# SwiGLU and output products of a decoder layer: 512 weight columns moved past stationary activations, inner rows transposed on TensorE, residual stream and norms token-major

## The chip, the cores and the metric

One core of a Trainium2 chip runs the kernel. The metric is the time of one execution on the device in microseconds (us), the median of three runs. The names used below: TensorE (PE in the profile) multiplies matrices, with PEld for its loads of the stationary operand; VectorE (DVE), ScalarE (ACT) and GpSimd (POOL) work element by element; SyncE (SP) issues the DMA transfers, in order, from one queue.

## What is computed

One decoder layer on 256 tokens of width 2048, conditioned on a vector c, everything in f32:

```
cond = silu(c);  mod = cond @ ada_w + ada_b          # nine vectors of 2048: shift, scale, gate, three times
h = rmsnorm(x)*g*(1+sc1) + sh1
x = x + 0.5*gt1 * swiglu(h, gate, up, down)          # inner width 5632
h = rmsnorm(x)*g*(1+sc2) + sh2
x = x + gt2 * (mixer(h) @ w_out)                     # 8 attention heads, 8 gated delta rule heads
h = rmsnorm(x)*g*(1+sc3) + sh3
x = x + 0.5*gt3 * swiglu(h, gate, up, down)
out = rmsnorm(x)*final_norm
swiglu(h, wg, wu, wd) = (silu(h @ wg) * (h @ wu)) @ wd
```

## The kernel before

**Weights.** All weight matrices are cut into 5392 tiles of 128x128 and packed on the host in the order in which the kernel uses them. The class `Stream` brings eight tiles at a time: a block of 512 KB by DMA (L91), ScalarE's cast to a rounded part `whi` (L93), and VectorE's difference `wlo` (L105). Three blocks of each kind are in memory, and in the SwiGLUs every fourth block lies in a buffer of its own. A product of weights and activations is three products of such parts: hi with hi, hi with lo, lo with hi.

**Feature-major layout.** The residual stream `x` lies with features on partitions: 16 slices of 128 features, 256 tokens each. `hs` holds the modulated input in the same layout, hi and lo beside each other. A weight tile is the stationary operand, and the tokens move past it: `mm` (L380 to 382) moves 512 columns (hi and lo of 256 tokens) past `whi`, then 256 past `wlo`; the output bank holds hi in its first half and the lo product in its second, and `merge` (L384) adds the halves with a ScalarE copy and a VectorE addition. The first part of the first SwiGLU (`gate_up_first`, L449 to 451) and the mixer's `project` (L623 to 625) move 256 columns three times for each tile and need no merge. Only `project_rows` in the mixer (L636 to 638, tile `pv`) has the other form: 128 tokens of `hs` stationary, 512 weight columns moving.

**Stages.** The first SwiGLU runs in two parts of 28 and 16 slices of the inner width (`PARTS`), each with gate and up (`pgu`, then `pg` and `pu`) and down (`pd`); the mixer with its projections (`pp`, `pv`) and small products; the output projection (`po`); the second SwiGLU in two parts of 22 and 22. The inner rows `hid` come out of gate and up feature-major, as down needs them.

**Conditioning.** The nine vectors `mod` are made column by column (128 features, 1 MB of weights, called an ada column here) by one VectorE product and sum (L233). `Stream.next` calls for such a column at a pace that the table `RATE` gives for each block number.

**Residual and norms.** `residual` (L405, L406) adds a 128-feature slice, scaled with its gate column. `sumsq_add` squares it on ScalarE and sums on GpSimd; `norm_rstd` (L282 to 309) sums over partitions with TensorE (`nsum`), takes a root and one refining step, and spreads the result over a row with TensorE (`nrow`). `modulate_one` (L313) then makes `hs`, slice by slice, `AHEAD` of the products. `final` scales 16 slices and stores them.

The framework's scheduler sets each engine's order from the program's order and its own estimates; transfers are tied to the last weight block by `issue_after(W.last)`.

Of the kernel before, what the change touches and what calls it, by code (L numbers as in the profile page):

```python
# [22 lines left out]
PARTS = ((0, 28, NF), (0, NF // 2, NF))  # L23
CHUNKS = (0, 2, 8, 16)
LEAD = (2, 5, 5)
NH = 8
# [7 lines left out]
RATE = ((0, 0.5), (24, 0.34), (56, 0.45), (68, 0.06), (112, 0.5), (168, 0.38), (264, 0.1), (280, 0.25), (408, 0.125))  # L34
# [6 lines left out]
HIDX = 3  # L41
# [4 lines left out]
MAGIC = 0x5F3759DF  # L46

# [3 lines left out]
for _k, _w in (  # L51
    ("foxm", 384), ("mL", 128), ("mU", 128), ("zm", 2 * 64), ("blk", 4), ("id16", 16),
    ("tri", 128), ("tri64", 128), ("tru64", 128), ("sgn", GR),
):
    CST[_k] = (_n, _w)
    _n += _w
# [12 lines left out]
class Stream:  # L69


    def __init__(self, nc, w, raw, hi, lo):
# [6 lines left out]
        self.at, self.first = {}, []  # L79

# [14 lines left out]

    def next(self, mat, k, n, width=1):
        i = len(self.order)
        if i % WB == 0:
# [7 lines left out]
            if b in self.at:  # L106
                self.at.pop(b)()
# [11 lines left out]
def layer_kernel(ctx: ExitStack, tc: tile.TileContext, xt, xrow, c, adaw, cols, cst, w, out, order, dbg=None):  # L119
# [67 lines left out]
    for b, sl in X_LATE.items():  # L187
        W.at[b] = lambda sl=sl: x_late(*sl)
# [16 lines left out]
    mod = keep.tile([P, 9 * KD], F32, name="mod")  # L205
# [6 lines left out]
    def ada_col():  # L212
# [56 lines left out]
    def sumsq_add(j):  # L269

        if j == 0:
            sqa["acc"] = tmp.tile([P, T], F32, name="sqacc", bufs=1)
            A.activation(sqa["acc"], x[:, j], AF.Square)
            return
        s = tmp.tile([P, T], F32, name="sq")
        A.activation(s, x[:, j], AF.Square)
        if j == KD - 1:
            sqa["src"] = [sqa["acc"], s]
        else:
            G.tensor_tensor(sqa["acc"], sqa["acc"], s, ALU.add)  # L280

    def norm_rstd(keep_row=False):  # L282

        ps = psf("nsum")
        src = sqa["src"]
        for i, s in enumerate(src):
            for t in range(2):
                PE.matmul(ps[:, t * 2 : t * 2 + 2], s[:, t * P : (t + 1) * P], L("ones", 0, 2),
                          start=(i == 0 and t == 0), stop=(i == len(src) - 1), skip_group_check=True)
        y = tiny.tile([P, 2], F32, name="nstd")  # L290
        hv = tiny.tile([P, 2], F32, name="nhv")
        ya = tiny.tile([P, 2], F32, name="nya")
        A.activation(y, ps[:, 0:4:2], AF.Sqrt, bias=L("eps"), scale=1.0 / D)
        V.tensor_scalar(hv, ps[:, 0:4:2], -0.5 / D, -0.5 * EPS, ALU.mult, ALU.add)
        V.reciprocal(y, y)
        V.tensor_tensor(ya, y, y, ALU.mult)
        V.tensor_tensor(ya, ya, hv, ALU.mult)
        V.scalar_tensor_tensor(y, ya, 1.5, y, ALU.add, ALU.mult)
        rb = tmp.tile([P, 2, P], F32, name="rb", bufs=1)
        pr = psf("nrow")  # L300
        for t in range(2):
            last = V.tensor_scalar(rb[:, t], L("ones"), y[:, t : t + 1], None, ALU.mult)
            PE.matmul(pr[:, t * P : (t + 1) * P], rb[:, t], ident, start=True, stop=True)
        W.held = ([None, sqa["hold"]] if sqa["hold"] is not None else []) + [last.ins]
        if not keep_row:
            return pr[:, :T]
        row = tmp.tile([P, T], F32, name="nrow", bufs=1)
        V.tensor_copy(row, pr[:, :T])
        return row

    hs = keep.tile([P, KD, 2, T], F32R, name="hs")

    def modulate_one(j, g1, sh, r):  # L313

        t = pt("ht")
# [17 lines left out]
    def modulate(which, m_sh, m_sc):  # L333
        ada_need(max(m_sh, m_sc), KD - 1)
        g1 = gains(which, m_sc, 0, KD)
        r = norm_rstd()
        hq["next"], hq["one"] = 0, lambda j: modulate_one(
            j, g1[:, j : j + 1], mod[:, m_sh * KD + j : m_sh * KD + j + 1], r)
# [872 lines left out]
```

## Time and profile before

| what | us |
|---|---|
| median of the runs | 2098.63 (2095.85 to 2101.67) |
| profiled execution, span | 2101.9 |
| first SwiGLU, up to the gap ahead of the mixer | 0 to 789.1 |
| mixer projections | 795.4 to 1223.2 |
| output projection | 1223.2 to 1331.6 |
| second SwiGLU | 1338.6 to 2085.7 |
| end | 2085.7 to 2101.9 |

The profile of one execution gives the span from the first to the last instruction; the execution's own time outside it isn't given apart, and the span stands 3.3 us above the median. The page shows busy time for each engine, the chain that ended last, and groups of instructions by line and tile; the trace can be asked for stretches and for single instructions with their starts. Starts of neighbouring matmuls say more than their durations, since matmuls overlap.

### The profile page before, as it was taken

Reading aid. Unit: us, or ns where it says so; the run is one execution under the profiler, and the core shown is the slowest. Engines: PE = TensorE matmul, PEld = TensorE weight load, DVE = VectorE, ACT = ScalarE, POOL = GpSimd, SP = SyncE. Lnnn points to the kernel's source line nnn. Section 1 sums busy time; section 2 is a strip of 40 time slices with the busy share of each in tenths; the row PEclk is TensorE's granted clock in tenths of the full one; section 3 lists DMA queues with packets and bytes.
Section 4 is the critical chain, followed back from the end, with each engine's and each line's share of the span. In section 5 each row is a group of like instructions: output and inputs, shape, how many; then the busy total and the mean of one; then the engine's idle time right before and its main releaser. Section 6 shows DMA issues by size and latency. Waiting matters only on the chain.

```text
span 2101.9 us, 33335 instructions
## 1 busy us (share of the span) xinstructions
PE 2037.6 (97%) x12935; PEld 1825.4 (87%) x12935; DVE 1564.1 (74%) x2393; ACT 1014.9 (48%) x1583; POOL 65.0 (3%) x58
## 2 busy tenths in 40 slices
PE   7999999999999999889999999999999999999997
PEld 5999999888888888779989978788888888888886
DVE  6898977888888988877878878866666555555554
ACT  5534544333444446646656654554444334444442
POOL 0000000000000120000000002000000000000011
PEclk9999999999999999999999999999999999999998
DMA  9988767999888875776666567666676555555553
GB/s 385 330 306 317 284 209 258 362 341 362 333 328 335 324 290 175 209 253 212 223 226 231 200 217 279 207 237 232 235 238 219 186 185 191 184 187 191 185 186 111
DMA packets 130064, 523.36 MB, mean 249 GB/s; under 512 B 16489, under 2 KB 21609, under 8 KB 111729
## 3 DMA queue, kind: packets, MB, share of 16 engines
q1 hardware_dynamic: 129906, 521.23, 69.7%
q8 instruction: 102, 1.67, 0.3%
q14 instruction: 56, 0.46, 0.1%
HBM read 516.83 MB, written 4.34 MB: 248 GB/s over the span
## 4 chain that ended last, share of the span: by engine, by line
PE 89%; DVE 5%; DMA 3%; issue 1%; ACT 1%; SPq 0%; DVEq 0%; POOL 0%; ACTq 0%; POOLq 0%
PE pd L381 15%; PE pu L381 11%; PE pg L381 11%; PE pd L382 8%; PE pg L382 5%; PE pu L382 5%; PE pgu L451 5%; PE pgu L449 5%; PE pgu L450 4%; PE pp L623 3%; PE pp L625 3%; PE pp L624 3%; PE po L381 2%; DVE wlo L105 2%; DMA adat<-in_ada_dram 1%
## 5 line engine op out<-in xcount | busy, mean ns | idle before, releaser
L105 DVE TENSOR_TENSOR wlo<-wraw,whi 128x1024 fp32r<-128x1024 f32 x674 | 823.7, 1228 | 344.0 <-ACT whi L93 341.4
L93 ACT CAST whi<-wraw 128x1024 fp32r<-128x1024 f32 x674 | 701.7, 1047 | 682.2 <-issue 173.7
L381 PE MATMUL pd<-hid,whi 128*128 128x512 f32 x1408 | 497.0, 397 | 0.0
L382 PE MATMUL pd<-hid,wlo 128*128 128x256 f32 x1408 | 396.0, 281 | 0.8 <-DVE wlo L105 0.7
L233 DVE CUSTOM_DVE_ANT_0 adat<-adat,cs,colt 128x2048 f32<-128x2048 f32 x140 | 329.7, 2355 | 29.3 <-DMA adat<-in_ada_dram 29.1
L381 PE MATMUL pg<-hs,whi 128*128 128x512 f32 x960 | 342.5, 397 | 2.3 <-DVE hs L324 1.8
L381 PE MATMUL pu<-hs,whi 128*128 128x512 f32 x960 | 343.2, 398 | 0.0
L381 PEld LDWEIGHTS pd<-hid,whi 128*128 128x128 f32 x1408 | 264.2, 188 | 64.7
L382 PE MATMUL pg<-hs,wlo 128*128 128x256 f32 x960 | 270.6, 282 | 0.0
L382 PE MATMUL pu<-hs,wlo 128*128 128x256 f32 x960 | 270.2, 281 | 0.0
L382 PEld LDWEIGHTS pd<-hid,wlo 128*128 128x128 f32 x1408 | 265.4, 189 | 2.5 <-DVE wlo L105 2.1
L449 PE MATMUL pgu<-hs,whi 128*128 128x256 f32 x896 | 252.6, 285 | 9.1 <-ACT hs L319 4.6
L451 PE MATMUL pgu<-hs,wlo 128*128 128x256 f32 x896 | 250.7, 285 | 3.9 <-DVE wlo L105 3.9
L450 PE MATMUL pgu<-hs,whi 128*128 128x256 f32 x896 | 253.1, 284 | 0.0
L381 PEld LDWEIGHTS pg<-hs,whi 128*128 128x128 f32 x960 | 181.0, 188 | 45.8 <-issue 2.1
L381 PEld LDWEIGHTS pu<-hs,whi 128*128 128x128 f32 x960 | 180.9, 188 | 43.8
L623 PE MATMUL pp<-hs,whi 128*128 128x256 f32 x656 | 193.0, 295 | 6.9 <-ACT whi L93 5.8
L625 PE MATMUL pp<-hs,wlo 128*128 128x256 f32 x656 | 188.9, 288 | 1.7 <-DVE wlo L105 1.7
L624 PE MATMUL pp<-hs,whi 128*128 128x256 f32 x656 | 189.1, 288 | 0.0
L382 PEld LDWEIGHTS pg<-hs,wlo 128*128 128x128 f32 x960 | 181.9, 190 | 0.0
L382 PEld LDWEIGHTS pu<-hs,wlo 128*128 128x128 f32 x960 | 181.9, 189 | 0.0
L449 PEld LDWEIGHTS pgu<-hs,whi 128*128 128x128 f32 x896 | 172.0, 193 | 10.8 <-ACT hs L319 5.0
(304 smaller groups left out, 2422.3 us busy)
## 6 DMA issues: line engine op xcount, KB each, us to landing
wraw<-in_w_dram SPq DMA_DIRECT2D x674, 512.0 KB, 4.3
adat<-in_ada_dram SPq DMA_DIRECT2D x140, 1024.0 KB, 6.6
rw<-rowd SPq DMA_DIRECT2D x24, 128.0 KB, 6.7
xr<-in_xr_dram SPq DMA_DIRECT2D x4, 512.0 KB, 5.2
adaf<-in_ada_dram SPq DMA_DIRECT2D x4, 512.0 KB, 9.3
adaf<-in_ada_dram SPq DMA_DIRECT2D x2, 1024.0 KB, 12.9
xd<-x SPq DMA_DIRECT2D x4, 512.0 KB, 6.7
x<-ld SPq DMA_DIRECT2D x16, 128.0 KB, 6.1
```

The costliest lines, as they stand in the source:

```text
L93: self.cast = self.nc.scalar.copy(self.h, r).ins
L105: nc.vector.tensor_tensor(self.l, r, self.h.bitcast(F32), ALU.subtract)
L233: V.tensor_tensor_reduce(t, t, cs, 1.0, L("adab", q, 1), ALU.mult, ALU.add, mod[:, q : q + 1])
L381: PE.matmul(ps, wt[0], act.rearrange("p a t -> p (a t)"), start=first, stop=False)
L382: PE.matmul(ps[:, :T], wt[1], act[:, 0], start=False, stop=last)
L449: PE.matmul(o, wh, hs[:, k, 0], start=first and s == 0, stop=False, skip_group_check=skip)
L450: PE.matmul(o, wh, hs[:, k, 1], start=False, stop=False, skip_group_check=skip)
L451: PE.matmul(o, wl, hs[:, k, 0], start=False, stop=last, skip_group_check=skip)
L623: PE.matmul(pp[i][:, :T], wh, hs[:, k, 0], start=(k == 0), stop=False)
L624: PE.matmul(pp[i][:, :T], wh, hs[:, k, 1], start=False, stop=False)
L625: PE.matmul(pp[i][:, :T], wl, hs[:, k, 0], start=False, stop=(k == KD - 1))
```

## The change

The residual stream `x` becomes token-major: 128 tokens on partitions, twice 2048 features. In the SwiGLUs and the output projection, 128 tokens of activations are now stationary and 512 weight columns (four tiles) move; `products` issues six matmuls for it, three for each half t of the tokens. Gate and up give token-major inner rows, so `turned` transposes them with TensorE, eight 128x128 transposes for four slices, `STEPS_BEHIND` products later, and splits them into hi and lo. `down` puts the first half of the tokens `SKEW` slices ahead in the last pass before a norm. The residual works on 512 features of one token half with a gate row `gtr`, which goes from the columns `mod` through DRAM (`row_send`, `row_load`). Sums of squares come from ScalarE's accumulator, token by token, and `modulate` scales, transposes (`pxt`) and modulates. The mixer's `project` takes `mm` and `merge`. The gates' rates and parts change (`RATE` from block 68 on, second SwiGLU in 24 and 20 slices), `x` is loaded again token-major (`x_rows`), and tables are padded so that tiles start at other addresses (`pad`, `SHIFT`). `final` scales four 512-wide pieces for each half.

```diff
-PARTS = ((0, 28, NF), (0, NF // 2, NF))
+PARTS = ((0, 28, NF), (0, 24, NF))
+LATER_LEAD = 4
+STEPS_BEHIND = 4
+SKEW = 2
+SHIFT = 8
-RATE = (..., (68, 0.06), ...)
+RATE = (..., (68, 0.15), ...)
...
+    hbuf = keep.tile([P, KD * 2 * T + 32], F32R, name="hs")
+    hview = [hbuf[:, o : o + KD * 2 * T].rearrange("p (k a t) -> p k a t", k=KD, a=2) for o in (0, SHIFT)]
...
+    def row_send(m, b):
+        g, f = ROW[m]
+        gs = tiny.tile([P, 4], F32, name="gs")
+        V.tensor_scalar(gs, mod[:, m * KD + 4 * b : m * KD + 4 * b + 4], f, None, ALU.mult)
+        with tc.issue_after(W.last):
+            nc.sync.dma_start(gdram[g, 4 * b : 4 * b + 4].rearrange("j p -> p j"), gs)
+    def row_load(m, b):
+        src = gdram[ROW[m][0], 4 * b : 4 * b + 4].rearrange("j p -> (j p)").unsqueeze(0).to_broadcast([P, 512])
+        with tc.issue_after(W.last):
+            nc.sync.dma_start(gtr[:, 512 * b : 512 * b + 512], src)
...
+    def norm_rstd(t):
+        A.activation(y, col(3), AF.Sqrt, bias=col(6), scale=1.0 / D)
+        V.scalar_tensor_tensor(hv, col(3), -0.5 / D, col(5), ALU.mult, ALU.add)
         V.reciprocal(y, y)
+        V.scalar_tensor_tensor(ya, y, hv, y, ALU.mult, ALU.mult)
         V.scalar_tensor_tensor(y, ya, 1.5, y, ALU.add, ALU.mult)
...
+        def one(j):
+            if j % 2 == 0:
+                st["ps"] = psf("pxt")
+                for t in range(2):
+                    xn = tmp.tile([P, T], F32, name="xn", bufs=4)
+                    if t:
+                        last = V.tensor_scalar(xn, X(t, j * P, T), y[t], None, ALU.mult)
+                    else:
+                        A.activation(xn, X(t, j * P, T), AF.Copy, scale=y[t])
+                    for q in range(2):
+                        o = q * T + t * P
+                        PE.transpose(st["ps"][:, o : o + P], xn[:, q * P : (q + 1) * P], ident)
...
+    def residual(ps, t, b, m_gt, squares):
+        row_need(m_gt, b)
+        sl = slice(512 * b, 512 * b + 512)
+        d = tmp.tile([P, 512], F32, name="rs")
+        V.tensor_tensor(d, ps, gtr[:, sl], ALU.mult)
+        sqa["hold"] = V.tensor_tensor(X(t, 512 * b, 512), X(t, 512 * b, 512), d, ALU.add).ins
+        if squares:
+            square(t, b)
...
+    def products(ps, hi_, lo_, wt, first, last, both=(0, 1)):
+        wh, wl = wt
+        for t in both:
+            PE.matmul(ps[t], hi_(t), wh, start=first, stop=False)
+            PE.matmul(ps[t], lo_(t), wh, start=False, stop=False)
+        for t in both:
+            PE.matmul(ps[t], hi_(t), wl, start=False, stop=last)
+        step()
...
+        def turned(c, src):
+            pz = [bank("pz") for _ in range(2)]
+            for t in range(2):
+                for q in range(4):
+                    PE.transpose(pz[t][:, q * P : (q + 1) * P], src[:, t, q * P : (q + 1) * P], ident)
+            h4 = hid[c] = hp.tile([P, 4, 2, T], F32R, name="hid", tag="hid")
+            for t in range(2):
+                A.copy(h4[:, :, 0, sl], pv)
+                V.tensor_tensor(h4[:, :, 1, sl], pv, h4[:, :, 0, sl].bitcast(F32), ALU.subtract)
...
-                wh, wl = W.next(m, k, n)
-                PE.matmul(pp[i][:, :T], wh, hs[:, k, 0], start=(k == 0), stop=False)
-                PE.matmul(pp[i][:, :T], wh, hs[:, k, 1], start=False, stop=False)
-                PE.matmul(pp[i][:, :T], wl, hs[:, k, 0], start=False, stop=(k == KD - 1))
+                mm(pp[i], W.next(m, k, n), hs[:, k], k == 0, k == KD - 1)
...
+        for t in range(2):
+            y = norm_rstd(t)
+            V.scalar_tensor_tensor(X(t, 1536, 512), X(t, 1536, 512), y, cs[:, 1536:], ALU.mult, ALU.mult)
+            A.activation(X(t, 0, 512), X(t, 0, 512), AF.Copy, scale=y)
+            V.tensor_scalar(X(t, 512, 512), X(t, 512, 512), y, None, ALU.mult)
+            A.activation(X(t, 1024, 512), X(t, 1024, 512), AF.Copy, scale=y)
+            for b in (0, 3, 1, 2):
+                nc.sync.dma_start(out[:, t, 512 * b : 512 * b + 512], X(t, 512 * b, 512))
```

How it stands on the engines, first on TensorE in the gate products of the second SwiGLU, before. The row gives line, operation, output, then the moving and the stationary operand, and the moving size (numbers tell buffers apart):

```order
L382 MATMUL pg_19850<-hs_128,wlo_19856 128x256
L381 MATMUL pg_19850<-hs_128,whi_19854 128x512
L382 MATMUL pg_19850<-hs_128,wlo_19856 128x256
L381 MATMUL pg_19850<-hs_128,whi_19854 128x512
L382 MATMUL pg_19850<-hs_128,wlo_19856 128x256
```

The same place in the changed kernel, where a group's inner rows `sg` are transposed into `pz` between two products; two `pgu` banks hold the token halves:

```order
L511 MATMUL pgu_12761<-whi_12783,hs_88 128x512
L512 MATMUL pgu_12761<-whi_12783,hs_88 128x512
L511 MATMUL pgu_12762<-whi_12783,hs_88 128x512
L512 MATMUL pgu_12762<-whi_12783,hs_88 128x512
L514 MATMUL pgu_12761<-wlo_12785,hs_88 128x512
L514 MATMUL pgu_12762<-wlo_12785,hs_88 128x512
L533 MATMUL pz_12799<-colt_93,sg_12607 128x128 x4
L533 MATMUL pz_12800<-colt_93,sg_12607 128x128 x4
L511 MATMUL pgu_12761<-whi_12816,hs_88 128x512
```

Two rows for each tile became six for four tiles, weights and activations changed places, and a batch of eight transposes stands between two products. Now VectorE between the first SwiGLU and the mixer, before (`nsum` and `rb` belong to the norm, `ht` and `hs` to the modulation):

```order
L405 SCALAR_TENSOR_TENSOR x<-pd,gh,x 128x256
L406 SCALAR_TENSOR_TENSOR x<-pd,gh,x 128x256
L105 TENSOR_TENSOR wlo<-wraw,whi 128x1024
L294 TENSOR_SCALAR nhv<-nsum 128x2
L295 RECIPROCAL nstd<-nstd 128x2
L296 TENSOR_TENSOR nya<-nstd 128x2
L297 TENSOR_TENSOR nya<-nya,nhv 128x2
L298 SCALAR_TENSOR_TENSOR nstd<-nya,nstd 128x2
L302 TENSOR_SCALAR rb<-colt,nstd 128x128 x2
L105 TENSOR_TENSOR wlo<-wraw,whi 128x1024
L316 SCALAR_TENSOR_TENSOR ht<-x,g_8163,nrow 128x256 x3
```

And in the changed kernel, from the last addition of the first token half on (`xn` is what TensorE transposes):

```order
L483 TENSOR_TENSOR x<-x,rs 128x512
L482 TENSOR_TENSOR rs<-pd,gtr 128x512
L358 SCALAR_TENSOR_TENSOR nhv<-ss 128x1
L359 RECIPROCAL nstd<-nstd 128x1
L483 TENSOR_TENSOR x<-x,rs 128x512
L360 SCALAR_TENSOR_TENSOR nya<-nstd,nhv 128x1
L113 TENSOR_TENSOR wlo<-wraw,whi 128x1024
L361 SCALAR_TENSOR_TENSOR nstd<-nya,nstd 128x1
L358 SCALAR_TENSOR_TENSOR nhv<-ss 128x1
L359 RECIPROCAL nstd<-nstd 128x1
L360 SCALAR_TENSOR_TENSOR nya<-nstd,nhv 128x1
L361 SCALAR_TENSOR_TENSOR nstd<-nya,nstd 128x1
```

The second half's addition to `x` moved behind the first half's reciprocal, a weight block's split stands inside the chain of small steps, and another follows after the first scalings.

More of the change, by code (lines that the diff above doesn't have):

```diff
@@ L40 @@
 TILE_US = 0.35
-HIDX = 3
 MORE = True
@@ L267, in sqrt_table, with square @@
         return A.activation(d, after, AF.Sqrt, scale=0.0)
[L269 to L294, printed above, removed]
+    def square(t, b):
+        j1 = tmp.tile([P, 512], BF16, name="jq")
+        A.activation(j1, X(t, 512 * b, 512), AF.Square, accum_out=ss[:, t, b : b + 1])
+        if b == 2:
+            V.tensor_reduce(ss[:, t, 4:5], ss[:, t, 0:3], mybir.AxisListType.X, ALU.add)
+            V.tensor_scalar(ss[:, t, 5:6], ss[:, t, 4:5], -0.5 / D, -0.5 * EPS, ALU.mult, ALU.add)
+            V.tensor_scalar(ss[:, t, 6:7], ss[:, t, 4:5], 1.0 / D, EPS, ALU.mult, ALU.add)
@@ L298, in norm_rstd @@
         V.scalar_tensor_tensor(y, ya, 1.5, y, ALU.add, ALU.mult)
[L299 to L311, printed above, removed]
+        return y
     def modulate_one(j, g1, sh, r):
+        hs = hview[0]
         t = pt("ht")
@@ new lines, in layer_kernel, with bank, step @@
+    turn = [0]
+    def bank(name):
+        turn[0] += 1
+        return psn(turn[0], name)
+    behind = []
+    def step():
+        for e in behind:
+            e[0] -= 1
+        while behind and behind[0][0] <= 0:
+            behind.pop(0)[1]()
+    def products(ps, hi_, lo_, wt, first, last, both=(0, 1)):
[6 more added lines that the diff above has]
+        step()
@@ new lines, in down @@
+    def down(which, f0, f1, hid, m_gt, squares):
+        fs = list(range(f0, f1))
+        for b in range(4):
+            row_need(m_gt, b)
+            ps = (bank("pd"), bank("pd"))
+            lag = SKEW if b == 3 and squares else 0
+            held = []
+            part = lambda f, a: lambda t: hid[f // 4][:, f % 4, a, t * P : (t + 1) * P]
+            for f in fs:
+                wt = W.next(("d", which), f, 4 * b, 4)
+                held.append((f, wt))
+                products(ps, part(f, 0), part(f, 1), wt, f == f0, f == f1 - 1, (0,) if lag else (0, 1))
+                if lag and len(held) > lag:
+                    g, wt = held.pop(0)
+                    products(ps, part(g, 0), part(g, 1), wt, g == f0, False, (1,))
+            if lag:
+                residual(ps[0], 0, b, m_gt, squares)
+                for g, wt in held:
+                    products(ps, part(g, 0), part(g, 1), wt, g == f0, g == f1 - 1, (1,))
+                residual(ps[1], 1, b, m_gt, squares)
+            else:
+                for t in range(2):
+                    residual(ps[t], t, b, m_gt, squares)
+            if squares and b == 2:
+                W.quiet = True
+        W.quiet = False
```

335 lines of the change are left out of this document (175 added, 160 removed).

## The prediction

> **What bounds the kernel now.** I read the page's busy shares and its chain that ended last first, then a table of stretches, then single instructions of TensorE in order of time.
>
> ```profile
> PE 2037.6 (97%) x12935; PEld 1825.4 (87%) x12935; DVE 1564.1 (74%) x2393; ACT 1014.9 (48%) x1583; POOL 65.0 (3%) x58
> PE 89%; DVE 5%; DMA 3%; issue 1%; ACT 1%; SPq 0%; DVEq 0%; POOL 0%; ACTq 0%; POOLq 0%
> ```
>
> TensorE is busy for 97% of the span and carries 89% of the chain. A busy TensorE says nothing of its rate, so I cut the span into stages. The columns are the stretch, its length, busy time with count for PE, PEld, DVE, ACT and POOL, then granted clock, DMA share and GB/s.
>
> ```profile
> 20.00:100.00 80.00, 72.93 (x576) 70.61 (x576) 65.98 (x72) 41.67 (x60) 0.00 (x0) 0.98 0.95 361
> 100.00:232.00 132.00, 128.10 (x1048) 127.69 (x1049) 120.35 (x139) 55.91 (x62) 0.00 (x0) 0.97 0.86 316
> 232.00:358.90 126.90, 126.90 (x1068) 126.90 (x1067) 100.43 (x161) 63.42 (x97) 0.00 (x0) 1.00 0.67 228
> 358.90:518.80 159.90, 159.09 (x898) 137.20 (x897) 140.03 (x158) 59.60 (x58) 0.00 (x0) 1.00 0.96 356
> 518.80:789.10 270.30, 270.30 (x1540) 235.69 (x1538) 233.10 (x278) 123.63 (x177) 21.73 (x14) 1.00 0.86 322
> 795.40:1223.20 427.80, 410.71 (x2935) 378.68 (x2936) 343.81 (x802) 263.76 (x543) 0.63 (x2) 0.97 0.63 215
> 1338.60:2085.70 747.10, 746.62 (x4224) 649.67 (x4225) 449.39 (x581) 340.61 (x476) 18.23 (x14) 1.00 0.58 199
> ```
>
> The last row is the whole second SwiGLU: 4224 matmuls, two for each 128x128 weight tile, so 2112 tiles in 747.1 us, 0.354 us a tile, with nothing else in the way. The rows from 358.9 to 789.1 (rest of the first SwiGLU, 1216 tiles) give 430.2 us, again 0.354. Only from 20 to 100, and from 358.9 to 518.8, is DMA nearly full (0.95, 0.96). What a tile costs is read from the starts of neighbouring matmuls.
>
> ```profile
> 1499.89 0.40 PE L381 MATMUL pg<-hs,whi 128*128 128x512 f32 x1
> 1500.13 0.28 PE L382 MATMUL pg<-hs,wlo 128*128 128x256 f32 x1
> 1500.25 0.40 PE L381 MATMUL pg<-hs,whi 128*128 128x512 f32 x1
> ...
> 252.38 0.28 PE L449 MATMUL pgu<-hs,whi 128*128 128x256 f32 x1
> 252.50 0.28 PE L450 MATMUL pgu<-hs,whi 128*128 128x256 f32 x1
> ...
> 1083.42 0.39 PE L636 MATMUL pv<-whi,hs 128*128 128x512 f32 x1
> ...
> 1084.78 0.39 PE L636 MATMUL pv<-whi,hs 128*128 128x512 f32 x1
> ```
>
> A 512-column matmul followed by a 256-column one holds TensorE 0.24 us, the 256 after it 0.12: 0.36 here, 0.354 on average. Three of 256 (first part of the first SwiGLU, and the mixer's `pp`) take 3 x 0.12 = 0.36. The `pv` rows are the form that the change spreads everywhere: stationary `hs`, 512 moving weight columns. From 1083.42 to 1084.78 there are six starts, 0.2267 us each.
>
> **The change, part by part.** All three forms move 768 columns for one tile; the new one does so in 1.5 instructions and not in two or three. Six `pv`-like matmuls for four tiles cost 6 x 0.2267 / 4 = 0.340 us a tile. All terms are against the profiled span, 2101.9 us.
>
> (a) 3328 tiles of rows 358.9 to 789.1 and 1338.6 to 2085.7: 1177.4 us become 3328 x 0.340 = 1131.5: **-45.9**.
>
> (b) 896 tiles up to 358.9: 0.36 to 0.340 is -17.9. Until 100 us DMA sets the pace, and until 232 VectorE is busy 120.35 of 132 us; I give back 6 us there: **-12**.
>
> (c) From 358.9 to 518.8, 448 tiles would need 152.3 us. 356 GB/s at a share of 0.96 is 371 at 1.0, and the 56.9 MB moved there need at least 153.5 us. I give back **+4**, for transfers that do not fill every gap.
>
> (d) 256 output tiles, 0.354 to 0.340: **-3.6**. (e) The mixer's 656 `pp` tiles go from three 256s (0.36) to 512 plus 256 (0.354): **-3.9**.
>
> (f) Transposes are new: 8 for each group of four inner rows, 22 groups, 176; and 64 for the two norms.
>
> ```profile
> 919.28 0.27 PE L833 MATMUL pvq<-colt,qv 128*128 128x128 f32 x1
> 919.39 0.27 PE L834 MATMUL pvq<-colt,qv 128*128 128x128 f32 x1
> ...
> 919.72 0.61 PE L837 MATMUL pkq<-qv,kk 128*128 128x128 f32 x4
> ```
>
> Four f32 transposes in a row take 919.28 to 919.72, 0.11 us each: 176 x 0.11 = **+19.4**. Of the 64, eight for each norm stand in its gap (g), the other 48 cost **+5.3**. The Trainium skill, "TensorE: Matmul & The Clock Gate", section "Part 4: PE-mode transpose", has about 275 ns for one in a kernel; 176 of these would be an estimate of 48 us and a total near 2087, but the 0.11 us of the rows is this kernel's, and decides. That a batch waits for its input is hidden by four products (4 x 1.36 us) between the last product of a group and its transposes; in this time VectorE has two 512-wide steps for the group (four in the first part of the first SwiGLU), 1.4 to 2.8 us, besides a weight block's split of 1.23 us.
>
> (g) The two norms. TensorE has nothing to do between the last product and the first `hs`.
>
> ```profile
> 789.10:795.40 6.30, 2.41 (x14) 1.94 (x12) 5.48 (x14) 1.22 (x4) 1.32 (x5) 0.67 0.59 217
> 2085.70:2101.90 16.20, 2.38 (x14) 1.92 (x12) 9.37 (x21) 2.57 (x7) 4.41 (x5) 0.58 0.34 129
> ```
>
> The durations are those of the groups by line: line, engine, operation and tiles with the count, then busy time and mean in ns, then the wait ahead of them.
>
> ```profile
> L464 DVE TENSOR_TENSOR acc<-pgu,acc 128x512 f32<-128x512 f32 x28 | 19.2, 687 | 3.0 <-PE pgu L451 2.9
> L462 ACT COPY acc<-pgu 128x512 f32<-128x512 f32 x28 | 16.3, 587 | 13.4 <-PE pgu L451 12.8
> L105 DVE TENSOR_TENSOR wlo<-wraw,whi 128x1024 fp32r<-128x1024 f32 x674 | 823.7, 1228 | 344.0 <-ACT whi L93 341.4 <-PE pp L625 0.9
> ```
>
> New path for the second half of the tokens: two 512-wide VectorE steps (0.69 each, as L464), a square (0.59, as L462), a root, four small steps, one scaling, two transposes, modulation. The row sums and the row broadcast on TensorE go. But the last addition stands behind the first half's reciprocal, and two splits of weight blocks (1.23 us) stand in VectorE's order between. About 7.8 us and not 6.3: **+1.5 each, +3**. TensorE's clock was 0.67 in this gap, and stays low as long.
>
> (h) The end takes 16.2 us.
>
> ```profile
> 2088.27 0.26 ACT L293 ACTIVATE nstd<-nsum,colt 128x2 f32<-128x2 f32 x1
> 2088.55 0.16 DVE L294 TENSOR_SCALAR nhv<-nsum 128x2 f32<-128x2 f32 x1 [1.60 <-ACT nstd L293]
> ...
> 2091.47 6.78 DVE L1088 SCALAR_TENSOR_TENSOR o<-x,colt,nrow 128x256 f32<-128x256 f32 x11
> ```
>
> Root (0.26) and small steps (0.16) come first; eleven scalings (6.78 us) follow a row broadcast, and 3.65 us pass from their end (2098.25) to the end. In their place: matmul drain 0.39, two 0.69 steps with two small ones between (1.7), square 0.59, root and four small steps 0.9, four 512-wide scalings on two engines 1.4, then the same 3.65 and hand-overs: about 9. **-7**.
>
> Costed at nothing: 41 `merge`s in the mixer, since VectorE and ScalarE are busy 343.8 and 263.8 of 427.8 us.
>
> ```profile
> L389 DVE TENSOR_TENSOR tg<-pg,mg 128x256 f32<-128x256 f32 x60 | 25.1, 419 | 2.2 <-ACT mg L388 2.0
> L388 ACT COPY mg<-pg 128x256 f32<-128x256 f32 x60 | 22.1, 368 | 35.6 <-PE pg L382 35.6
> ```
>
> They add 41 x 0.419 = 17 us to VectorE and 41 x 0.368 = 15 to ScalarE; without the cover at most 17 us. Also at nothing, by the waits of SP's own queue between 358 and 519 us (total, times, longest):
>
> ```profile
> SPq L231 <- DVE mod L233: 44.8, 20, 5.5
> ```
>
> Twelve pieces of the gate rows go to DRAM and back, and the token rows (2 MB) are loaded again. These sit on SP's queue, in order, and each send waits for a VectorE step, with the next weight blocks queued behind it. A like wait (an ada column's transfer, for VectorE) was 5.5 us at its longest; three blocks in flight are 8 us of products, which hides it. Four sends in the first SwiGLU without cover would be 22 us. Lighter evacuation (one 512-wide step where two 256-wide ones stood) is off the path and gains nothing.
>
> Sum: -45.9 - 12 + 4 - 3.6 - 3.9 + 19.4 + 5.3 + 3 - 7 = -40.7, so a span of 2061.2. The timed runs have a median of 2098.63, 3.3 below the profiled span; carried over: **2058 us**.
>
> The bound on the main term is wide. 512 columns can hold TensorE no less than the step from 256 to 512 shows ((0.2267 - 0.12) x 2 = 0.213 us), and 0.24 is what the 512s of `pg` take: 4480 tiles make -92 and +90 us of it. I take 0.2267, since `pv` is the same form, every start of it at that distance.
>
> **The rivals.**
>
> *Columns alone set the price* (slower). Then the product gains vanish, since the columns stay the same, and transposes, norms and end remain: +19.4 + 5.3 + 3 - 7 = +20.7, less 3.3: **2119**. The place is every product of the SwiGLUs; a 512 that takes 0.24, as beside `pg`, goes that way. It decides above 0.2267 + 40.7 / 6720 = 0.2327 us per matmul. Against it: `pv`. In the Trainium skill, "TensorE: Matmul & The Clock Gate", section "Back-to-back issue gap" has columns / 2.4 + 2.5 ns for a warm isolated gap; as an estimate that is 0.325 us a tile before and 0.324 after, so it is this rival's rule. The trace disagrees: 0.12 us, not 0.109, for 256.
>
> *The intake becomes the bound in the first SwiGLU.* If DMA and VectorE hold the pace until 789 us, the gains of 1216 tiles (16.7) and of (b) go, and (c)'s 4 falls away: **2083**. The 0.96 speaks for it, the 0.86 after 518.8 against it.
>
> *Shorter still.* If pairing hindered `pv` too and a 512 takes 0.222, 6720 x 0.0047 = 32 us more go: **2026**.
>
> *The mixer pays for its merges:* **2075**.
>
> **How the numbers follow.** Forecast 0.58, columns alone 0.10, intake 0.12, shorter 0.13, mixer 0.07. The range 2025 to 2094 leaves out the columns rival and half of the shorter one, with some of the edges. A difference of 0.3%, 6 us, is about what can be told from none. Faster: 0.57 + 0.11 + 0.13 + 0.06, near 0.86; slower 0.10; the same 0.04.
>
> **What would show it.** Starts of `pgu` and `pd` matmuls 0.227 apart; second SwiGLU near 718 us plus 88 transposes (10 us); DMA share 0.96 or more from 350 to 500; eight `pz` starts in 0.9 us; gaps near 8 us at the norms, 9 at the end. Starts 0.235 apart, or waits for `wlo` in the first SwiGLU or for `sg` at the transposes, would prove it wrong.

## The result and the profile after

The changed kernel takes 2148.75 us (median, 2148.34 to 2159.72) against 2097.24 for the kernel before in the same comparison: a ratio of 1.025, 95% interval 1.0225 to 1.0276. The forecast was 2058 us, faster. Its profiled execution has a span of 2146.9 us, 85.7 above the span that the prediction worked out (2061.2).

From the page after: the busy shares, the chain that ended last, and ScalarE's cast of the weight blocks with the idle time ahead of it.

```profile
PE 2038.0 (95%) x9347; PEld 1654.3 (77%) x9347; DVE 1487.1 (69%) x2085; ACT 989.6 (46%) x1420; POOL 2.2 (0%) x11
PE 81%; DMA 7%; DVE 6%; ACT 3%; issue 2%; SPq 0%; ACTq 0%; DVEq 0%; POOLq 0%
L97 ACT CAST whi<-wraw 128x1024 fp32r<-128x1024 f32 x674 | 704.4, 1052 | 922.8 <-DMA wraw<-in_w_dram 343.7
```

TensorE is as busy as before, with 9347 instructions and not 12935, but DMA has gone from 3% of the chain to 7%. The cast waits 343.7 us for weight blocks, against 142.6 before. That row of the waits before (total, times, longest):

```profile
ACT whi L93 <- DMA wraw<-in_w_dram: 142.6, 68, 7.6
```

Next the same stages as before the change: stretch, length, busy time with count for PE, PEld, DVE, ACT and POOL, granted clock, DMA share, GB/s.

```profile
232.00:359.70 127.70, 125.48 (x564) 103.01 (x565) 100.88 (x111) 59.58 (x69) 0.00 (x0) 0.99 0.76 246
359.70:542.30 182.60, 164.11 (x682) 131.16 (x681) 135.54 (x127) 59.89 (x58) 0.00 (x0) 0.95 0.93 328
542.30:814.80 272.50, 269.19 (x1184) 218.92 (x1184) 210.35 (x205) 109.41 (x124) 0.00 (x0) 1.00 0.82 309
814.80:824.60 9.80, 2.41 (x11) 1.48 (x9) 8.07 (x22) 6.96 (x15) 1.34 (x5) 0.63 0.15 23
824.60:1263.40 438.80, 411.72 (x2303) 342.77 (x2303) 352.28 (x837) 275.84 (x571) 0.62 (x2) 0.97 0.63 218
1263.40:1283.80 20.40, 14.61 (x76) 10.96 (x74) 13.20 (x46) 7.73 (x25) 0.00 (x0) 0.83 0.47 160
1283.80:1380.10 96.30, 91.93 (x388) 73.09 (x387) 62.77 (x77) 40.58 (x54) 0.00 (x0) 0.98 0.70 247
1386.90:2136.10 749.20, 744.01 (x3282) 608.62 (x3280) 398.69 (x397) 314.45 (x348) 0.00 (x0) 0.99 0.59 196
2136.10:2146.90 10.80, 0.35 (x2) 0.00 (x0) 4.62 (x14) 4.23 (x10) 0.00 (x0) 0.76 0.52 194
```

Set beside the prediction's terms, each stage cut at the start of its first product (its transposes put where they stand: 48 and 8 in the first two rows, 32 in the third, 88 in the second SwiGLU, 24 of the norms' after each gap), with two of the kernels of the experiments:

| stage, us | before | predicted | after | without row transfers (e3) | rows on TensorE, solve's queue, banks, offset (e12) |
|---|---|---|---|---|---|
| gate-up, first part, from 19.8 | 339.1 | 332.4 | 339.9 | 336.3 | 336.6 |
| down, first part | 159.9 | 157.2 | 182.6 | 161.2 | 157.2 |
| rest of the first SwiGLU | 270.3 | 264.6 | 272.5 | 274.2 | 271.2 |
| norm gap | 6.3 | 7.8 | 9.8 | 6.9 | 6.8 |
| mixer and output | 536.1 | 531.2 | 555.5 | 551.0 | 539.7 |
| norm gap | 7.0 | 8.5 | 6.8 | 6.8 | 6.8 |
| second SwiGLU | 747.1 | 730.4 | 749.2 | 740.9 | 734.9 |
| end | 16.2 | 9.2 | 10.8 | 11.2 | 11.3 |

Three rows are far off: down of the first part (25.4 over the prediction), mixer and output (24.3), the second SwiGLU (18.8).

**The price of a product.** Starts of single instructions in order of time, from the second SwiGLU after the change: transposes, gate-up, then down.

```profile
1985.32 0.60 PE L533 MATMUL pz<-colt,sg 128*128 128x128 f32 x4
...
1989.88 0.39 PE L511 MATMUL pgu<-whi,hs 128*128 128x512 f32 x1
1990.11 0.39 PE L512 MATMUL pgu<-whi,hs 128*128 128x512 f32 x1
...
1991.24 0.39 PE L511 MATMUL pgu<-whi,hs 128*128 128x512 f32 x1
...
2100.12 0.40 PE L511 MATMUL pd<-whi,hid 128*128 128x512 f32 x1
2100.36 0.39 PE L512 MATMUL pd<-whi,hid 128*128 128x512 f32 x1
...
2101.52 0.40 PE L511 MATMUL pd<-whi,hid 128*128 128x512 f32 x1
```

These six `pgu` products take 1989.88 to 1991.24, 0.2267 each: the predicted price to the digit. These six `pd` products take 2100.12 to 2101.52, 0.2333 each, 0.350 us a tile and not 0.340. Over all products whose starts lie less than 0.26 us apart, the mean distance is 0.2287 in `pgu`, 0.2319 in `pd` and 0.2324 in `po`, so gate-up misses the price too, by less. Four transposes show 0.60 us busy, like the four of the prediction (0.61); a whole batch of eight takes 1.03 us in the median from the product before it to the one behind it, 0.10 for each transpose.

**The stall in down.** What SyncE issued around the third gate row's send (start, length, queue, line, transfer):

```profile
384.92 0.38 SPq L285 DMA_DIRECT2D gd<-gs  x1
385.40 0.92 SPq L95 DMA_DIRECT2D wraw<-in_w_dram  x2
386.37 0.42 SPq L254 DMA_DIRECT2D adat<-in_ada_dram  x1
386.89 0.37 SPq L95 DMA_DIRECT2D wraw<-in_w_dram  x1
394.24 0.33 SPq L291 DMA_DIRECT2D gtr<-gd  x1
```

Behind the send of 2 KB three weight blocks and an ada column (2.5 MB) were issued by 387. Then the queue stood until the send had landed, at 394.24. Two more views of the same place: the waits of SP's queue from 359 to 545 (total, times, longest), and TensorE in order of time.

```profile
SPq L291 <- DMA gd<-gs: 22.5, 3, 8.4
SPq L285 <- DVE gs L283: 12.7, 2, 7.8
```

```profile
391.82 0.64 PE L514 MATMUL pd<-wlo,hid 128*128 128x512 f32 x2
399.34 0.80 PE L511 MATMUL pd<-whi,hid 128*128 128x512 f32 x1 [6.88 <-ACT whi L97]
```

And stretches within it, columns as above:

```profile
386.00:396.00 10.00, 6.46 (x28) 4.87 (x26) 3.59 (x3) 0.36 (x1) 0.00 (x0) 1.00 1.01 34
...
400.00:402.00 2.00, 2.00 (x6) 1.59 (x5) 1.82 (x3) 0.56 (x1) 0.00 (x0) 0.50 0.97 402
```

From 386 to 396 the DMA engines are busy by their records (1.01) and move 34 GB/s, a tenth of the stage's 328. So the queue's wait is not all of it: the transfers that had been issued did not move either. And when TensorE starts again its granted clock is 0.50: products start 0.43 us apart (399.93, 400.36) and not 0.23; the six of the row count those that reach into it. The stall is paid once and its clock again. How much, the rows say beside those of the kernel without row transfers (e3 below): the same 682 instructions keep TensorE busy for 164.1 us and not 157.1, and the waits for `whi` and `wlo` are 18.5 us (13.7 and 4.8) and not 4.1. That is 7.0 and 14.4 of the 21.4 us between them. The Trainium skill, "TensorE: Matmul & The Clock Gate", Part 1, has the clock go to half after an idle window of about 3.4 us; the trace agrees for this stall, whose 6.88 us end at a clock of 0.50. It doesn't fit every one: a wait of only 2.0 us at 503 was followed by 0.50 from 507 to 509, too.

### The profile page after: what moved, and what is told of

Its sections match the earlier page's. It is cut to its first block, busy times and chain, and to the rows that moved or that the text cites. A ratio compares the mean times of both kernels' runs of the same rounds, so it can differ in the third digit from the quotient of the medians.

```text
span 2146.9 us, 25417 instructions
## 1 busy us (share of the span) xinstructions
PE 2038.0 (95%) x9347; PEld 1654.3 (77%) x9347; DVE 1487.1 (69%) x2085; ACT 989.6 (46%) x1420; POOL 2.2 (0%) x11
## 4 chain that ended last, share of the span: by engine, by line
PE 81%; DMA 7%; DVE 6%; ACT 3%; issue 2%; SPq 0%; ACTq 0%; DVEq 0%; POOLq 0%
PE pgu L514 14%; PE pgu L511 14%; PE pgu L512 14%; PE pd L514 7%; PE pd L511 7%; PE pd L512 7%; PE pp L460 5%; DMA wraw<-in_w_dram 4%; PE pp L461 3%; DVE wlo L113 3%; DMA adat<-in_ada_dram 2%; PE pv L758 1%; PE pv L759 1%; PE pv L757 1%; DVE adat L256 1%
## 5 line engine op out<-in xcount | busy, mean ns | idle before, releaser
L97 ACT CAST whi<-wraw 128x1024 fp32r<-128x1024 f32 x674 | 704.4, 1052 | 922.8 <-DMA wraw<-in_w_dram 343.7
L511 PE MATMUL pgu<-whi,hs 128*128 128x512 f32 x1408 | 556.4, 397 | 11.8 <-ACT hs L371 6.6
L512 PE MATMUL pgu<-whi,hs 128*128 128x512 f32 x1408 | 551.4, 393 | 5.2 <-DVE hs L415 5.2
L514 PE MATMUL pgu<-wlo,hs 128*128 128x512 f32 x1408 | 440.2, 394 | 5.1 <-DVE wlo L113 4.9
L511 PEld LDWEIGHTS pgu<-whi,hs 128*128 128x128 f32 x1408 | 267.0, 190 | 73.1 <-ACT hs L371 7.5
L514 PEld LDWEIGHTS pgu<-wlo,hs 128*128 128x128 f32 x1408 | 265.2, 189 | 66.7 <-DVE wlo L113 9.0
L512 PEld LDWEIGHTS pgu<-whi,hs 128*128 128x128 f32 x1408 | 266.7, 190 | 62.3 <-DVE hs L415 5.6
L511 PE MATMUL pd<-whi,hid 128*128 128x512 f32 x704 | 281.5, 400 | 13.7 <-ACT whi L97 13.7
L512 PE MATMUL pd<-whi,hid 128*128 128x512 f32 x704 | 278.6, 396 | 0.0
L460 PE MATMUL pp<-hs,whi 128*128 128x512 f32 x656 | 239.9, 402 | 2.1 <-ACT xn L402 1.1
L514 PE MATMUL pd<-wlo,hid 128*128 128x512 f32 x704 | 228.6, 398 | 5.5 <-DVE wlo L113 5.5
L511 PEld LDWEIGHTS pd<-whi,hid 128*128 128x128 f32 x704 | 133.7, 190 | 47.1 <-ACT whi L97 14.6
L514 PEld LDWEIGHTS pd<-wlo,hid 128*128 128x128 f32 x704 | 133.3, 190 | 39.2 <-DVE wlo L113 8.3
L512 PEld LDWEIGHTS pd<-whi,hid 128*128 128x128 f32 x704 | 133.7, 190 | 29.9
L461 PEld LDWEIGHTS pp<-hs,wlo 128*128 128x128 f32 x656 | 124.9, 190 | 6.8 <-DVE wlo L113 5.5
L757 PE MATMUL pv<-whi,hs 128*128 128x512 f32 x128 | 53.2, 423 | 11.3 <-ACT whi L97 11.3
```

The costliest lines, as they stand in the source:

```text
L97: self.cast = self.nc.scalar.copy(self.h, r).ins
L460: PE.matmul(ps, wt[0], act.rearrange("p a t -> p (a t)"), start=first, stop=False)
L461: PE.matmul(ps[:, :T], wt[1], act[:, 0], start=False, stop=last)
L511: PE.matmul(ps[t], hi_(t), wh, start=first, stop=False)
L512: PE.matmul(ps[t], lo_(t), wh, start=False, stop=False)
L514: PE.matmul(ps[t], hi_(t), wl, start=False, stop=last)
```

## The experiments

Theories at the start: (1) SyncE's in-order queue stands for the gate rows' round trip; rivals: the intake is full there, or the send itself is dear. (2) The output products wait for banks behind the chains; rival: the merges delay the chains. All times are medians; each ratio is to the kernel before in the same comparison. Kernels that keep the sends as they are scatter by some 10 us from run to run, and so does their mixer: mixer and output take 555.5 us in the changed kernel, and 564.9 in e6 and 562.7 in e7, which leave the mixer's work alone.

### e1: the same rows, later

```
+ row_owed[m, j // 4] = [row_scale, row_send, row_load]      # scaling, send and load apart
+ ROW_STEPS = (1, 5, 11)                                     # blocks later; was (2, 5)
- row_need(m_gt, b)                                          # at the start of a pass of down
```

> Same twelve gate-row pieces, same bytes, same queue; only their steps are pulled apart: the scaling on VectorE one weight block after its last column, the send four blocks later, the load six blocks after the send, and the rows are asked for at the residual and not at the start of a pass. Theory (SyncE's queue stands still for the scaling and for the landing of the send, and the weight blocks stand behind it): the waits of SP for gs and for gd (12.7 and 22.5 us between 360 and 545) fall below 5 us, down of the first part goes from 182.6 to about 160 us, some 5 us go elsewhere, and the total is 2115 to 2128. Rival (the transfers in this stage are full, 0.96 before, and the new ones have no room): the stage stays above 178 and the total above 2142. Second rival (the send of 512 pieces of 4 bytes itself holds the DMA engines): the SP waits go but the stage stays above 172.

Measured: 2140.9 us, ratio 1.0187 (1.0163 to 1.0211). Down of the first part takes 173.5 us. SP's waits from 359 to 533, and a stretch after the third row's send:

```profile
SPq L96 <- DVE gs L284: 1.1, 2, 0.8
```

```profile
394.00:404.00 10.00, 8.21 (x36) 6.10 (x34) 4.29 (x4) 2.10 (x2) 0.00 (x0) 1.00 0.98 137
```

The waits for `gs` and `gd` are gone (35.2 us to 1.1), and the stage keeps 12 of its 21 us over e3. That is the second rival's mark (waits gone, stage above 172): the queue may be part of it, but the traffic still falls to 137 GB/s, here with the engines busy by their records.

### e2: the same rows from another queue

```
- nc.sync.dma_start(gdram[...], gs)      - nc.sync.dma_start(gtr[...], src)
+ nc.gpsimd.dma_start(gdram[...], gs)    + nc.gpsimd.dma_start(gtr[...], src)
```

> The sends and loads of the gate rows are issued from GpSimd's queue, all else as after. Theory (SyncE's in-order queue): same as the late rows, stage about 160, total 2115 to 2128, since a wait on GpSimd's queue holds no weight block. Rival (DMA full, or the send itself is dear): no gain, above 2142.

Measured: 2149.93 us, 1.0235 (1.0214 to 1.0256). The stage is 174.7 us, as in e1, but others grew (gate-up of the second part 181.4 to 189.7 us). No gain: the rival's result, and another sign that the queue is not the point.

### e3: no row transfers

Both `dma_start` lines go; `gtr` is set to 0.5 once, so this kernel leaves the gates out.

> Leaves out the transfers of the gate rows altogether (gtr is a constant 0.5 in their place, so the gates are not applied). It prices them: theory, total 2112 to 2125, within 5 us of the late rows; rival (the stage is bound by its intake, 56.9 MB at the rate of before, for other reasons): 2140 or more.

Measured: 2109.28 us, 1.0038 (1.0025 to 1.0051), just below the 2112 to 2125 expected and 32 us below e1, where 5 were expected: to send the rows later saves little of their price. Stretches: the stage, and the 10 us in which the changed kernel moved 34 GB/s.

```profile
356.10:517.30 161.20, 157.12 (x682) 126.75 (x681) 135.02 (x127) 59.24 (x58) 0.00 (x0) 1.00 0.90 353
386.00:396.00 10.00, 10.00 (x45) 8.10 (x44) 7.42 (x8) 3.39 (x4) 0.00 (x0) 1.00 1.00 380
```

The rows cost 38.7 us of span (2146.9 to 2108.2): 21.4 in this stage, 8.3 in the second SwiGLU, 4.5 in the mixer, the rest at the start and in the norm gap.

### e6, e14 and e15: what in the send is dear

All three leave the loads out, and with them the gates.

```
e6    nc.sync.dma_start(gdram[g, 4*b : 4*b+4].rearrange("j p -> p j"), gs)       # 512 x 4 bytes, neighbours
e14   gd [3, 4, P, 4]:        nc.sync.dma_start(gdram[g, b], gs)                 # 128 x 16 bytes
e15   gd [3, KD, P, 128]:     ...(gdram[g, 4*b : 4*b+4, :, 0]...)                # 512 x 4 bytes, 512 bytes apart
```

> The sends of the gate rows stay as they are, the loads are left out (gtr is a constant 0.5, so the gates are not applied). Theory (the send holds the engines): most of the price stays, 2128 to 2145, and packets of weight blocks still last 7 us or more. Rival (SyncE's wait for the landing, or the load, is the price): within 5 us of the kernel without rows, 2104 to 2115.

> As e6_send_only (loads left out, gtr a constant 0.5, so the gates are not applied), but each partition's four values go out side by side: 128 pieces of 16 bytes in place of 512 of 4, the same 2 KB. Theory (the number of pieces): landing falls from 10.6 to about a quarter, 2 to 4 us, and total to 2112 to 2125. Rival (any write to DRAM among the weight blocks holds the engines): landing 8 us or more and total above 2140.

> As e6_send_only, 512 pieces of 4 bytes, but each goes to a place of its own, 512 bytes from the next, where in e6_send_only neighbouring partitions write neighbouring 4 bytes. Theory (neighbouring pieces write into the same short stretch of DRAM and wait for each other): landing 2 to 5 us and total 2112 to 2128. Rival (the number of pieces alone): landing 9 us or more as before, total above 2140.

Measured: e6 2158.33 us, 1.0275 (1.0253 to 1.0297); e14 2107.83, 1.0049 (1.0032 to 1.0066); e15 2110.97, 1.0058 (1.0041 to 1.0075). The times from issue to landing of the twelve sends in e6, e14 and e15, in this order:

```profile
DMA to landing us min/median/max: 10.0/10.6/13.6
```

```profile
DMA to landing us min/median/max: 1.4/3.3/6.4
```

```profile
DMA to landing us min/median/max: 1.9/3.1/5.6
```

And the 10 us from the third send on (issued at 385.65, 378.76 and 377.27; landed after 10.6, 2.9 and 3.3 us), in the same order:

```profile
385.65:395.65 10.00, 9.69 (x42) 7.51 (x40) 4.51 (x4) 1.05 (x1) 0.00 (x0) 1.00 0.16 31
```

```profile
378.76:388.76 10.00, 10.00 (x45) 8.12 (x44) 7.35 (x6) 3.30 (x4) 0.00 (x0) 1.00 0.72 267
```

```profile
377.27:387.27 10.00, 10.00 (x45) 8.11 (x44) 7.08 (x6) 3.16 (x3) 0.00 (x0) 1.00 0.91 337
```

The send alone has the whole price: with the loads gone the time is no lower (e6 came out above its range, on the theory's side). And e15 has the same 512 pieces of 4 bytes and the same 2 KB, only 512 bytes apart in DRAM, and the price is gone: 3.1 us to landing in the median and 337 GB/s behind the third. So it is not the number of pieces alone (e15's rival falls). It is not neighbourhood alone either, since the 16-byte pieces of e14 lie side by side too: what is dear is 512 pieces of 4 bytes side by side. Whether their number or their size counts there, no run separates.

Nor is it the wait of SyncE's queue for the scaling ahead of the send, which e14 and e15 both keep (from 360 to 520, the same row in each):

```profile
SPq L285 <- DVE gs L283: 12.3, 2, 7.6
```

The packets show what it does to the weight blocks. Packets of 4096 bytes last 0.16 us in the median; behind the sends some last up to 9.0 us in the changed kernel and 10.7 in e6, while none lasts 3 us before the change, nor in e3, e5, e14 and e15. Why they are held no view shows, and the engines' busy share doesn't help: it is 1.01 in the changed kernel and 0.16 in e6, with as few bytes moved. The Trainium skill, "DMA: Bandwidth & Descriptors", section "Why small descriptors are slow (HBM only)", has about three cycles for each packet and 32 bytes of metadata for each transfer; that would be an estimate far below a microsecond on 16 engines, and the trace of e6 disagrees (10.6 us).

### e5: rows without a transfer

```
+ pg = bank("pgr")
+ for q in range(4):
+     PE.transpose(pg[:, q*P : (q+1)*P], mod[:, o+q : o+q+1].to_broadcast([P, P]), ident)
+ A.activation(gtr[:, 512*b : 512*b+512], pg, AF.Copy, scale=f)
```

> The gate rows are made without any transfer: four transposes of a broadcast gate column on TensorE give a row of 512 in all partitions, and one ScalarE copy scales it into gtr. Theory (each send of 512 pieces of 4 bytes holds the DMA engines for about 9 us, with the weight blocks among them): as fast as the kernel without rows plus 48 x 0.11 = 5.3 us of transposes at most, 2108 to 2118; down of the first part near 162 us; no 4096-byte packet over 3 us. Rival (the gain without rows came from the residual not having to wait for a row): 2130 or more.

Measured: 2113.84 us, 1.0069 (1.0054 to 1.0085), in the range; down of the first part takes 160.5 us, and no 4096-byte packet lasts over 2.2 us. The rows can be had on TensorE for about 4 us of span over e3 (2112.0 against 2108.2).

### e4 and e8: the mixer

```
e4    + turn[0] = 7                       # ahead of the output products: banks psb, psb, psb, pss
e8    pp: three PE.matmul of 256 columns for each tile, as before the change; no merge in gates, conv_silu and fox
```

> Only the count behind the bank choice is set ahead of the output products, so that their first four banks are three of psb and one of pss, as before the change, and not two of psf and two of pss, which the two chains still use. Theory (output products wait behind the chains' tail for a bank, and TensorE has 20 us of nearly nothing from 1263 to 1284): mixer and output together go from 555.5 to 535 to 541, total 2128 to 2135. Rival (the chains run late because of the merges on VectorE and ScalarE, so that the output products would wait for the last heads anyway): both stay within 5 us, 2143 or more.

> Only the mixer's projections go back to three products of 256 columns without merge. By the starts in the two traces, a tile then costs 0.360 and not 0.347 us: +8.5 us. Theory (the merges delay the chains, on ScalarE and VectorE): the early mixer loses its extra 12 us and the tail its extra 4 to 8, so mixer and output 540 to 550, total 2133 to 2143. Rival (the delay comes with the norm's transposes, the saved x and the transfers, not with the merges): 558 to 566 and 2151 or more.

Measured: e4 2158.49 us, 1.028 (1.0251 to 1.0309); e8 2166.6, 1.0328 (1.0303 to 1.0352). Stretches of e4 (output, now with the chains' last work in it), and of e8 (mixer and output):

```profile
1273.40:1387.30 113.90, 104.39 (x460) 81.01 (x459) 76.41 (x122) 48.12 (x77) 0.00 (x0) 0.97 0.67 233
```

```profile
828.90:1392.60 563.70, 525.53 (x3419) 464.00 (x3419) 421.62 (x924) 324.59 (x632) 0.62 (x2) 0.96 0.64 217
```

In e4 the 20.4 us of tail and 96.3 of output become 113.9, 2.8 us less, and mixer and output together stay at 556.8. I had taken the tail for nearly empty; its row above has TensorE busy for 14.6 of 20.4 us, so there was little to fill. e8 gives 563.7, inside its rival's 558 to 566 and far from the theory's 540 to 550: the merges are not what delays the mixer. It is 8 us longer than the changed kernel, as the starts say that the 512 and 256 form is worth (8.5), but with e6's 564.9 and e7's 562.7 beside it this comparison can't prove that.

### e7: hid at another address

```
- d = tiny.tile([P, 1], F32, name="dummy")
+ d = tiny.tile([P, 24], F32, name="dummy")[:, :1]       # hid and oh start 128 bytes later
```

> A small tile is made wider, so that hid and oh start 128 bytes later; nothing else. In after, starts of pd matmuls are 227 apart where the next stationary operand's address and the moving one's agree modulo 256 bytes, and mostly 229 or 237 where they are 128 apart; hid and the weight blocks are 128 apart in three blocks of four. Theory (that offset): pd starts at 227 to 228 everywhere, the four down stages together 8 to 12 us shorter, total 2137 to 2143. Rival (the PSUM bank or hid's own layout): pd stages within 2 us, total 2146 to 2152.

Measured: 2156.34 us, 1.0265 (1.0246 to 1.0283): no gain in all, and above both ranges. But down of the second SwiGLU's first part, in the changed kernel and then in e7:

```profile
1666.70:1801.20 134.50, 134.50 (x586) 109.03 (x585) 68.49 (x65) 51.48 (x51) 0.00 (x0) 1.00 0.55 188
```

```profile
1681.40:1812.80 131.40, 131.40 (x585) 108.90 (x584) 68.27 (x64) 51.61 (x50) 0.00 (x0) 1.00 0.62 191
```

Both hold 576 products and eight transposes: 0.232 and 0.2266 us a product. From 1667 us on, behind the last send, the stages are together 7.0 us shorter than in the changed kernel; stages with sends are longer by more (down of the first part 185.8 us and not 182.6, mixer and output 562.7 and not 555.5). That the scatter of the sends hides the offset's gain in the total is argued, not shown; so it was taken up again without sends.

The addresses that the built kernels give their tiles, set beside the starts, say more. In the changed kernel the mean distance of two products in `pd` is 0.2288 us where the next stationary operand and the moving one agree modulo 256 bytes, and 0.2329 where they are 128 bytes apart (three in four); in `pgu` 0.2274, and 0.2326 (one in four). In e7 all agree, and the mean is 0.2270 in `pgu` and 0.2269 in `pd`.

### e9, e10, e11, e12 and e13: together, without sends

e9 is e5 with e7's edit. e10 adds `nc.gpsimd` for the transfers of the mixer's two `solve` steps, e11 adds e4's `turn[0] = 7`. e12 is e11 with the small tile 32 wide, e13 is e12 with `STEPS_BEHIND = 7`.

> The gate rows made on TensorE and hid and oh moved by 128 bytes, together. In the moved kernel alone the pd stages after 720 were 1.5, 3.0 and 2.4 us shorter and gate-up 1.8, while the stages with sends varied by as much the other way. Theory (the offset was worth its 12 to 18 us, hidden there by stalls behind the sends): 2096 to 2103, that is 10 to 18 below the rows on TensorE alone (2113.8, or 1.0069 of before). Rival (the shorter products only lengthen waits for weight blocks): 2108 to 2116.

> As the kernel with rows on TensorE and hid moved, and the mixer's two solve steps send and load their blocks (ld) from GpSimd's queue and not from SyncE's. Theory (SyncE stands 8 to 10 us at the second solve, for VectorE, with the weight blocks of pv behind it, and TensorE then runs at half clock): the mixer loses 8 to 14 us, total 2084 to 2093. Rival (TensorE there waits for the solve itself, in order, not for weights): within 4 us of the kernel without this edit.

> As the one before, with the bank count set ahead of the output products again, now with no sends about. Theory (output products that fill the chains' tail are worth what they filled, some 6 us: 20.4 us of tail with 14.5 us of TensorE work in it): 3 to 7 us less. Rival (the tail's work is only moved): within 2 us or slower.

> As the kernel with rows on TensorE, solve on GpSimd's queue and the bank count, but hid and oh moved so that their offset against the weight blocks is 0 modulo 256 bytes; without the small gs tiles it had come out at 64 and 192, not at 0, in the three kernels before. Theory (offset): the second SwiGLU's two down stages go from 133.1 and 111.0 to 131 and 109.5, its gate-up by 2 to 3 us, all stages together 6 to 10 us; total 2093 to 2098. Rival (the shorter products only lengthen other waits): 2101 or more.

> As e12_offset_mended, and the transposes of a group of inner rows come seven products after its last one and not four. Theory (in the first SwiGLU they wait for VectorE's acc, 2.1 us at 230 us and as much near 316, and each such gap is followed by 3.4 us at half clock): 2 to 6 us less than e12_offset_mended. Rival (the first SwiGLU is paced by its weights there): within 1.5 us of it.

| kernel | us | ratio to before (95%) |
|---|---|---|
| e9 | 2109.08 | 1.0045 (1.0029 to 1.0062) |
| e10 | 2106.57 | 1.0033 (1.0020 to 1.0046) |
| e11 | 2103.17 | 1.0012 (1.0003 to 1.0022) |
| e12 | 2085.27 | 0.9927 (0.9907 to 0.9947) |
| e13 | 2089.98 | 0.9956 (0.9944 to 0.9968) |

e9 came out in its rival's range because its edit missed: without the two small `gs` tiles, `hid` came to lie 64 or 192 bytes off and not 0. With the offset at 0 in e12, six `pd` products take 1.36 us (1700.03 to 1701.39), and the second SwiGLU goes from 742.3 us in e11 to 734.9 (starts in order of time, then its stretch):

```profile
1700.03 0.39 PE L506 MATMUL pd<-whi,hid 128*128 128x512 f32 x1
1700.26 0.39 PE L507 MATMUL pd<-whi,hid 128*128 128x512 f32 x1
...
1701.39 0.39 PE L506 MATMUL pd<-whi,hid 128*128 128x512 f32 x1
```

```profile
1338.10:2073.00 734.90, 734.90 (x3297) 608.66 (x3296) 398.08 (x394) 317.16 (x352) 0.00 (x0) 1.00 0.60 199
```

The step from e11 to e12 is 17.7 us of span (2102.0 to 2084.3), more than the 6 to 10 expected: gate-up gains too, since the buffers of every fourth weight block moved with `hid`. By mean distances (`pgu` 0.2290 to 0.2270, `pd` 0.2298 to 0.2269, `po` 0.2289 to 0.2273) 15 of the 17.7 are TensorE's. e12 stands 0.7% below the kernel before, clear of its interval, and still 23.1 us of span above the predicted 2061.2. e10 was for SyncE's wait at the second `solve` (7.6 us in the changed kernel). TensorE's largest wait in the mixer, in e9 and then in e10:

```profile
PE pv L752 <- ACT whi L97: 15.6, 3, 9.1
```

```profile
PE pv L753 <- DVE wlo L113: 14.8, 5, 6.7
```

The wait for the weight block went, and a wait for its split on VectorE came in its place; 3.6 us were left of 8 to 14, the rival's result. e11 is 3.4 us lower in the median and 0.8 in mixer and output, so the banks matter little. e13 is slower than e12 by 4.7 us, outside both of its ranges; it gains 0.8 us in gate-up of the first part, where it was meant to, and loses 2.3 in down of the first part and 2.9 in the mixer, which its edit does not touch. Its theory also read too much into the clock: the wait near 230 us (1.8 us) is followed by half clock in e12 (0.51 from 234 to 236) and by full clock in e11 (1.00 from 231 to 237).

## Why the prediction was wrong, step by step

- **(a) 0.340 us a tile**: the mechanism was right, the size off. The mean distance is 0.2287 us in `pgu` and 0.2319 in `pd`, not 0.2267. What the prediction left out is the operands' place in memory: at the right offset (e12, 0.2270 and 0.2269) the second SwiGLU takes 734.9 us, and without its 88 transposes and 24 for the norm (12.3 us) 722.6 for 2112 tiles, 0.342. From the distances of the changed kernel and of e12, the error is an estimate of 20 us of the 85.7.
- **Gate rows at nothing, the step that failed most.** The prediction said that three blocks in flight, 8 us of products, hide a wait of SP's queue, and put 22 us on the case without cover. It priced the queue alone. The send stops the blocks in flight too (34 GB/s for 10 us), so the cover was not there: 38.7 us by e3, all of it the send by e6, and its 4-byte pieces side by side by e14 and e15.
- **(b), (c)** Gate-up of the first part gained 2.8 of 6.7 us once the rows are out (336.3 in e3 against 339.1), down 157.2 in e12, as forecast. The +4 given back in (c) was right without sends and at that offset (161.2 in e3, at the old one).
- **(d), (e), merges at nothing**: merges were rightly costed at nothing, as far as e8 shows: without them, and without (e), the mixer is no shorter. But mixer and output came to 551.0 in e3, not 531.2. Of these 20 us, 11 go with e5, e10, e11 and e12 together (539.7), of which the single edits carry 2.5 (e9, the half-mended offset), 3.6 (e10, solve's queue), 0.8 (e11, banks) and 4.4 (e12, offset). Some 8 us stay open. In e12 TensorE is busy for 513.0 us there, as before the change (410.7 and 102.3), and idle for 26.7 in place of 23.2; its largest wait is that of `pv` for the split of weight blocks, 13.6 us in five times. What keeps the busy time up was not tried.
- **(f) transposes**: 0.10 each, close to the forecast 0.11. Seven products of cover in place of four gain 0.8 us in gate-up of the first part (e13), so four hide nearly all of the wait (1.8 us, once, is left in e12).
- **(g), (h)**: the gaps were 9.8 and 6.8 in place of 7.8 and 8.5, 6.9 and 6.8 without sends; the end 10.8 in place of 9.2. Both were sized a little off, in opposite directions.
- **Rivals.** The columns rival has the right side (slower) and the wrong reason: starts of 0.2267 in `pgu`, and a mean of 0.2270 in e12, rule it out. The rival on intake had the right place (first SwiGLU, DMA) but took rate for the limit: the stage that was slowest moved fewer GB/s (328) than before (356), not more.

The sum closes in steps of span. Of the 85.7 us over the prediction, the row transfers are 38.7 (e3), of which rows made on TensorE give 3.8 back (e5). The two steps that move `hid` are 24.1 (e9 6.4, e12 17.7; one run each, so with their scatter), solve's queue 0.9 (e10) and the banks 2.7 (e11). The last 23.1 stand in e12 over the predicted column: 8.5 in mixer and output, 6.6 in the rest of the first SwiGLU, 4.5 in the second, 4.2 in gate-up of the first part and 2.1 at the end, less 2.7 in the norm gaps. They were not taken apart, and their cause stays open.

## What to carry to other kernels

Price a small transfer by what it does to the transfers beside it, not by its bytes or by its own queue: a column written into a row, 4 bytes from each partition side by side, all but stopped the weight stream for 10 us, and four transposes of a broadcast column gave the same row, twelve rows for 3.8 us in all. When the operands change places, look at their addresses again, since the same product cost 2 to 3% more at the wrong offset. And a stall of TensorE can be paid nearly one and a half times, once as a wait and once as clock: 14.4 and 7.0 us in down of the first part.

## What the runs showed of the hardware that was not expected

- Sends of 512 x 4 bytes to neighbouring places in DRAM: 10.6 us to landing in the median (e6), and 31 GB/s for all traffic in the 10 us from the third on. The same pieces 512 bytes apart (e15): 3.1 us and 337 GB/s. 128 pieces of 16 bytes (e14): 3.3 us and 267 GB/s.
- Products of 512 columns start 0.227 us apart on average where the next stationary operand and the moving one agree modulo 256 bytes in all of a kernel's SwiGLU products (e7, e12), and 0.233 where they are 128 apart (changed kernel). At 64 and 192 apart (e11) the second SwiGLU's first down stage stood between: 133.1 us, against 134.5 and 131.4. There `pd` has 0.230 at these offsets and at 0 alike, so the rule by single pairs is not clean; that the place of the operands moves the price is.
